# Low-part score products of a head pair contracted over 64 rows each, in a two-layer encoder trunk

## The chip, the cores and the metric

The kernel runs on one core of a Trainium2 chip. The metric is device time in microseconds (us) of one launch; the kernel before was timed three times. The profile is of one further execution, taken by the hardware profiler; its span runs from the first instruction to the last. Engines are named as the profile names them: PE is TensorE's matmuls and PEld its weight loads, DVE is VectorE, ACT ScalarE, POOL GpSimd, and SP the engine that issues most of the transfers.

## What is computed

The reference is a two-layer encoder trunk on 512 tokens of width 1024, in float32. Layer A mixes tokens with a four-head matrix memory (mLSTM) and with cross-attention to 256 memory tokens; layer B has chunked band attention with twelve heads of 64, and the same kind of memory cross-attention. Each layer ends with a gated MLP with a causal convolution. The change concerns the scores of the two attentions:

```python
def memory_attention(q, mem, w_kv):
    ...
    s = jnp.einsum('bshd,bmhd->bhsm', q, mk).astype(jnp.float32) * (MEM_HEAD_DIM ** -0.5)
    p = jax.nn.softmax(s, axis=-1).astype(mv.dtype)
    return jnp.einsum('bhsm,bmhd->bshd', p, mv).reshape(bsz, seq, MEM_WIDTH)

def band_attention(q, k_pad, v_pad, rel_table):
    ...
        s = jnp.einsum('bqhd,bkhd->bhqk', qc, kc).astype(jnp.float32) * scale + bias
        valid = (start - KV_PAD + kj) >= 0
        s = jnp.where(valid, s, -jnp.inf)
        p = jax.nn.softmax(s, axis=-1).astype(vc.dtype)
        return jnp.einsum('bhqk,bkhd->bqhd', p, vc)
```

Heads have 64 channels, so two heads share the 128 rows of a tile.

## The kernel before

**Numbers in two parts.** All products run on float32r operands. To keep float32's accuracy each operand x is held as a high part (x rounded to float32r) and a low part (x minus the high part). A full product of two operands a and b is then three matmuls into the same bank: high a with high b, high a with low b, low a with high b. mm3 (lines 176 to 180) does this; lines 178, 179 and 180 issue most of the kernel's matmuls.

**Scores of a head pair.** For 64-channel heads two of the three are put into one matmul of 128 rows. head_keys (line 504) makes for each head h a tile whose 64 rows of that head hold the high parts of the keys, and whose other 64 rows hold their low parts. head_queries (line 494) makes two tiles for each head. The first has the high parts of the queries in both halves, so that one matmul gives high times high plus high times low. The second has the low parts in the head's own rows; the other half is filled with zeros by GpSimd (line 497), so that a 128-row matmul adds low times high alone. HEADS is the pair of row ranges, 0 to 63 for head 0 and 64 to 127 for head 1. head_scores (line 511) issues the two matmuls of one head, at line 517; both load queries (or keys) as weights and accumulate in one PSUM bank.

**Who calls it.** scores (line 550) takes a head pair and two banks and calls head_scores for head 0, then for head 1: high and low of head 0, high and low of head 1. The softmax step of memory_attention (line 563) calls it for each of four tiles of 128 queries, with 256 keys; there are two head pairs in each of two layers. The softmax step of band_attention (line 1306) calls it for each of four query tiles with 128, 256, 384 and 512 keys; there are six head pairs. The mLSTM heads call head_scores themselves (line 1142), for one head at a time with the keys as weights, and need the 128-row form; their queries come from head_queries too, through qk_tile (line 1082). Attention queries come through queries (line 542).

**Order.** The kernel is written with generators: weave runs an attention job step by step and between its steps calls pieces of a filler (projections, output projection), so that other matmuls stand between the steps of a softmax. The final order on each engine is set when the program is compiled, by a planner that takes instructions in program order as far as what they need is there by its own estimate; a PSUM bank or a buffer that isn't free yet lets others go first. The engines then run their lists strictly as planned. PSUM tiles of the scores have three banks (tag sc); operand tiles have 57 buffers (tag u).

Of the kernel before, what the change touches and what calls it, by code (L numbers as in the profile page):

```python
# [46 lines left out]
def f(ap):  # L47
    return ap.bitcast(F32)
# [3 lines left out]
def trunk(  # L52
# [18 lines left out]
    nc = tc.nc  # L71
    V, A, G = nc.vector, nc.scalar, nc.gpsimd
# [10 lines left out]
    def sb(tag, shape, dtype=F32):  # L83
        count[0] += 1
        return pool.tile(shape, dtype, tag=tag, name=f"{tag}{count[0]}", bufs=bufs[tag])
# [28 lines left out]
    for i, sel in enumerate(sels):  # L114
        G.memset(f(sel), 0.0)
        for s in (2 * i, 2 * i + 1):
            q = slice(32 * s, 32 * s + AH)
# [11 lines left out]
    HEADS = (slice(0, HD), slice(HD, P))  # L129
# [3 lines left out]
    def split(hi, lo, src, on_act=True, pinned=False):  # L133
        high = A.copy(hi, src) if on_act else V.tensor_copy(hi, src)  # L134
        low = V.tensor_tensor(out=lo, in0=src, in1=f(hi), op=ALU.subtract)  # L135
        if pinned:
            pin(high)
            pin(low)
# [43 lines left out]
    def project(w, c0, act, tag="mm", lo=None):  # L182


        n = len(act)
        src = rows(w, c0, P)
        wh, wl = weights(src, n, P) if lo is None else summed_weights(lo, src, n, P)
        o = ps(tag)
        for k in range(n):
            mm3(o, wh[:, k, :], wl[:, k, :], act[k][0], act[k][1], k == 0, k == n - 1)  # L190
            yield
        return o
# [298 lines left out]

    def head_queries(t, scale=1.0):
        qs, ls = ([sb("u", [P, S], F32R) for _ in range(2)] for _ in range(2))
        for h, r in enumerate(HEADS):
            G.memset(f(ls[h])[HEADS[1 - h], :], 0.0)
            A.activation(qs[h][r, :], t[r, :], AF.Copy, scale=scale)
            V.scalar_tensor_tensor(ls[h][r, :], t[r, :], scale, f(qs[h])[r, :], op0=ALU.mult, op1=ALU.subtract)
        for h, r in enumerate(HEADS):  # L500
            A.copy(qs[h][HEADS[1 - h], :], f(qs[h])[r, :])
        return qs, ls

    def head_keys(t):
        ks = [sb("u", [P, S], F32R) for _ in range(2)]
        for h, r in enumerate(HEADS):
            A.copy(ks[h][r, :], t[r, :])
            V.tensor_tensor(out=ks[h][HEADS[1 - h], :], in0=t[r, :], in1=f(ks[h])[r, :], op=ALU.subtract)
        return ks

    def head_scores(o, h, q, tsl, k, c, first, keys_first=False):

        for i, part in enumerate(q):
            a, b = part[h][:, tsl], k[h][:, c]
            if keys_first:
                a, b = b, a
            nc.tensor.matmul(o, a, b, start=first and i == 0, stop=i == 1)  # L517
# [24 lines left out]
    def queries(o, row):  # L542

        if row is None:
            return head_queries(o, HD**-0.5)
        q = sb("t", [P, S])
        V.scalar_tensor_tensor(q, o, HD**-0.5, row, op0=ALU.mult, op1=ALU.mult)
        return head_queries(q)

    def scores(outs, q, tsl, k, c):  # L550

        for h in range(2):
            head_scores(outs[h], h, q, tsl, k, c, True)

    def memory_attention(q, kv, hp, mixes):

# [6 lines left out]
        def softmax(T2):  # L563
            ss = [ps("sc").rearrange("p (t m) -> p t m", t=2) for _ in range(2)]
            for i in range(2):
                T = 2 * T2 + i
                scores([s[:, i, :] for s in ss], q, slice(T * P, (T + 1) * P), k, slice(hp * MEM, (hp + 1) * MEM))
                yield
            for h in range(2):
                mx, sm = small(2), small(2)  # L570
                V.tensor_reduce(mx, ss[h], axis=AX.X, op=ALU.max, negate=True)
                e = sb("t", [P, S]).rearrange("p (t m) -> p t m", t=2)
                for i in range(2):
                    A.activation(e[:, i, :], ss[h][:, i, :], AF.Exp, bias=mx[:, i : i + 1], accum_out=sm[:, i : i + 1])
                V.reciprocal(sm, sm)
                for i in range(2):
                    V.tensor_scalar(e[:, i, :], e[:, i, :], sm[:, i : i + 1], None, op0=ALU.mult)
                es[T2, h] = e
                yield
# [417 lines left out]
    e, u, c, r = (cpool.tile([P, TT, AH], F32, name=f"gate{i}") for i in range(4))  # L997
# [84 lines left out]
    def qk_tile(c):  # L1082

        o = yield from project(w_in, c * P, act)
        acc = sb("t", [P, S])
        cw, cb = col["cw"], col["cb"]
        A.activation(acc, o, AF.Identity, scale=cw[:, 36 + c : 37 + c], bias=cb[:, c : c + 1])
        for i in (1, 2, 3):
            w = cw[:, 12 * (3 - i) + c : 12 * (3 - i) + c + 1]
            V.scalar_tensor_tensor(acc[:, i:], o[:, : S - i], w, acc[:, i:], op0=ALU.mult, op1=ALU.add)  # L1090
        A.activation(acc, acc, AF.Silu)
        if c % 3 == 1:
            return (head_queries if c < 6 else head_keys)(acc)
        hi, lo = sb("u", [P, S], F32R), sb("u", [P, S], F32R)
        split(hi, lo, acc)
        return hi, lo
# [14 lines left out]
    def a_tiles(*js):  # L1111
        for j in js:
            qs[j] = yield from qk_tile(j)
            ks[j] = yield from qk_tile(6 + j)
        for j in js:
            og[j] = yield from o_tile(j)
# [179 lines left out]
    def band_attention(j, q, k, v):  # L1296
# [9 lines left out]
        def softmax(T):  # L1306
            n = (T + 1) * P
            ss = [ps("sc")[:, :n] for _ in range(2)]
            scores(ss, q, slice(T * P, n), k, slice(0, n))
            for h in range(2):  # L1310
                e = sb("t", [P, S])[:, :n]
                mn, sm = small(1), small(1)
                V.tensor_tensor_reduce(
                    out=e, in0=ss[h], in1=biases[h][:, S - n :], scale=-1.0, scalar=BIG,
                    op0=ALU.add, op1=ALU.min, accum_out=mn,
                )
                A.activation(e, e, AF.Exp, bias=mn, scale=-1.0, accum_out=sm)
                V.reciprocal(sm, sm)
                V.tensor_scalar(e, e, sm, None, op0=ALU.mult)
                es[T, h] = e  # L1320
            yield
# [102 lines left out]
    for hf in range(2):  # L1424
# [6 lines left out]
        for Ts, pieces in groups:  # L1431
            for c in pieces:
                if c.start:
                    os_[Ts[0]] = ps("mm")
                for u in range(n):
# [4 lines left out]
                    for T in Ts:  # L1440
                        for i in range(2):
                            k = 2 * u + i
# [58 lines left out]
```

## Time and profile before

| what | value |
|---|---|
| median of three runs | 1211.98 us (1211.79 to 1214.2) |
| span of the profiled execution | 1209.9 us |
| matmuls at line 517 | 192, of which 160 by scores |
| memsets at line 497 | 24, of 64 x 512 elements |
| mean granted TensorE clock | 0.999 |

The page gives a line for each engine's busy time and for the chain of work that ended last. Queries of the trace give more: the busy time of each engine in stretches of the span; who waited for whom; a source line's instructions with their shortest, median and longest duration; and the timeline, where each row has its start, its duration, the engine, the line, the operation with out<-in by the program's names, the shape (rows*columns of the weights, then partitions x elements moved) and a count of merged instructions. Matmuls overlap in the pipeline, so their durations don't add up; from the start of one to the start of the next is what each costs a full TensorE.

### The profile page before, as it was taken

The numbers are of one execution on the slowest core, as the hardware profiler recorded it, in microseconds if no ns is written. First come the engines' busy times: TensorE is split into PE (matmuls) and PEld (weight loads), VectorE is DVE, ScalarE is ACT, GpSimd is POOL, SyncE is SP. The second block draws the span as 40 slices with busy tenths as digits, with TensorE's granted clock in tenths as the row PEclk, the third lists the DMA queues.
The fourth block names the chain that finished last, engine by engine and source line by source line (L and its number), as shares of the span: only waits on it lengthen the run. The fifth ranks groups of instructions, "written<-read, shape, count | busy, mean of one in ns | idle before, by whom it ended". The sixth has DMA issues, their size and how long they took to land.

```text
span 1209.9 us, 18791 instructions
## 1 busy us (share of the span) xinstructions
PE 1196.0 (99%) x7063; PEld 1058.6 (87%) x7063; DVE 945.1 (78%) x1733; ACT 711.1 (59%) x1251; POOL 125.3 (10%) x197
## 2 busy tenths in 40 slices
PE   9999999999999999999999999999999999999997
PEld 9988888888889999999988888878889999999986
DVE  7878688877978777777698888997896777777755
ACT  4536577644655555555475667775565555555545
POOL 1300000001011111111011000001101001111100
PEclk9999999999999999999999999999999999999999
DMA  8634111347556676665563323145845466666551
GB/s 276 207 98 122 54 53 57 109 138 187 129 137 160 145 160 150 161 141 133 143 195 109 99 72 94 57 129 167 199 97 139 107 138 139 140 140 134 120 156 70
DMA packets 205260, 159.14 MB, mean 132 GB/s; under 512 B 7960, under 2 KB 185586, under 8 KB 205170
## 3 DMA queue, kind: packets, MB, share of 16 engines
q1 hardware_dynamic: 184338, 120.78, 34.1%
q0 software_dynamic: 20832, 37.17, 16.5%
q8 instruction: 55, 0.90, 0.3%
q14 instruction: 35, 0.29, 0.1%
HBM read 129.42 MB, written 32.44 MB: 134 GB/s over the span
## 4 chain that ended last, share of the span: by engine, by line
PE 94%; ACT 3%; DVE 2%; issue 0%; ACTq 0%; DVEq 0%
PE pmm L178 18%; PE pmm L180 18%; PE pmm L179 18%; PE ptr L178 6%; PE ptr L179 6%; PE ptr L180 6%; PE psc L180 5%; PE psc L178 5%; PE psc L179 5%; PE psc L517 2%; PE ptr L1328 1%; ACT wh L134 1%; PE ptr L1349 1%; PE ptr L1350 1%; PE ptr L586 0%; PE ptr L600 0%
## 5 line engine op out<-in xcount | busy, mean ns | idle before, releaser
L178 PE MATMUL pmm<-u,wh 128*128 128x512 f32 (+1 forms) x968 | 337.1, 349 | 0.1
L180 PE MATMUL pmm<-u,wl 128*128 128x512 f32 (+1 forms) x968 | 333.6, 345 | 0.0
L179 PE MATMUL pmm<-u,wh 128*128 128x512 f32 (+1 forms) x968 | 333.3, 345 | 0.1
L135 DVE TENSOR_TENSOR wl<-wr,wh 128x1024 fp32r<-128x1024 f32 (+4 forms) x168 | 194.7, 1160 | 96.7 <-ACT wh L134 96.0
L134 ACT CAST wh<-wr 128x1024 fp32r<-128x1024 f32 (+4 forms) x168 | 168.0, 1002 | 99.9 <-PE pmm L179 47.2
L180 PEld LDWEIGHTS pmm<-u,wl 128*128 128x128 f32 x968 | 183.6, 190 | 21.1
L179 PEld LDWEIGHTS pmm<-u,wh 128*128 128x128 f32 x968 | 183.9, 190 | 18.0 <-DVE u L135 0.8
L178 PEld LDWEIGHTS pmm<-u,wh 128*128 128x128 f32 x968 | 183.7, 190 | 17.7 <-ACT u L134 0.5
L178 PE MATMUL ptr<-u,wh 128*128 128x512 f32 x272 | 106.7, 392 | 0.0
L179 PE MATMUL ptr<-u,wh 128*128 128x512 f32 x272 | 106.5, 392 | 0.0
L180 PE MATMUL ptr<-u,wl 128*128 128x512 f32 x272 | 105.8, 389 | 0.0
L748 POOL DMA_DIRECT2D xspill<-t x64 | 56.0, 875 | 411.4 <-ACT t L747 408.6
L178 PE MATMUL pmm<-u,u 128*128 128x256 f32 x296 | 84.5, 285 | 2.5 <-ACT t L824 2.5
L180 PE MATMUL pmm<-u,u 128*128 128x256 f32 x296 | 84.0, 284 | 0.4 <-DVE u L135 0.4
L179 PE MATMUL pmm<-u,u 128*128 128x256 f32 x296 | 83.8, 283 | 0.0
L135 DVE TENSOR_TENSOR u<-pt,u 128x512 fp32r<-128x512 f32 x102 | 69.9, 688 | 9.7 <-ACT u L134 7.1
L178 PE MATMUL psc<-u,wh 128*128 128x256 f32 (+1 forms) x232 | 76.1, 328 | 0.0
L179 PE MATMUL psc<-u,wh 128*128 128x256 f32 (+1 forms) x232 | 75.9, 327 | 0.0
L747 ACT COPY t<-ptr 128x512 f32<-128x512 f32 x64 | 37.5, 586 | 65.3 <-PE ptr L180 65.3
L135 DVE TENSOR_TENSOR u<-t,u 128x512 fp32r<-128x512 f32 x78 | 53.4, 689 | 21.4 <-ACT u L134 21.1
L134 ACT CAST u<-pt 128x512 fp32r<-128x512 f32 x102 | 63.2, 619 | 11.4 <-DVE pt L859 11.1
L921 ACT ACTIVATE t<-t 128x512 f32<-128x512 f32 x34 | 21.6, 635 | 80.2 <-DVE t L657 80.2
(290 smaller groups left out, 2568.0 us busy)
## 6 DMA issues: line engine op xcount, KB each, us to landing
wr<-in_ffn_w_up_dram SPq DMA_DIRECT2D x54, 512.0 KB, 5.0
wr<-in_ffn_w_down_dram SPq DMA_DIRECT2D x38, 512.0 KB, 3.8
pt<-in_ffn_w_up_dram SPq DMA_DIRECT2D x34, 512.0 KB, 6.8
xspill<-t POOLq DMA_DIRECT2D x64, 256.0 KB, 4.8
wr<-in_a_w_in_dram SPq DMA_DIRECT2D x20, 512.0 KB, 3.8
xspill<-u POOLq DMA_DIRECT2D x32, 256.0 KB, 3.0
u<-xspill SPq DMA_DIRECT2D x32, 256.0 KB, 4.9
wr<-in_w_kv_dram SPq DMA_DIRECT2D x12, 512.0 KB, 4.1
```

The lines of the kernel that those rows point to most:

```text
L134: high = A.copy(hi, src) if on_act else V.tensor_copy(hi, src)
L135: low = V.tensor_tensor(out=lo, in0=src, in1=f(hi), op=ALU.subtract)
L178: nc.tensor.matmul(o, lh, rh, start=first, stop=False, skip_group_check=more)
L179: nc.tensor.matmul(o, lh, rl, start=False, stop=False, skip_group_check=more)
L180: nc.tensor.matmul(o, ll, rh, start=False, stop=last, skip_group_check=more)
L517: nc.tensor.matmul(o, a, b, start=first and i == 0, stop=i == 1)
L747: A.copy(t, o)
L748: G.dma_start(xspill[j], t, accum_op=ALU.add)
L921: A.activation(self.acc, self.acc, AF.Silu)
L1328: nc.tensor.transpose(tp[:, b * P : (b + 1) * P], es[T, h][:, b * P : (b + 1) * P], ident)
L1349: nc.tensor.matmul(o2[:, s * P :], w, hi_at(pts[h], s, s, TT - s), start=s == 0, stop=False)
L1350: nc.tensor.matmul(o2[:, s * P :], w, lo_at(pts[h], s, s, TT - s), start=False, stop=s == TT - 1)
```

## The change

In scores the two high products now come first, on 128 rows as before, each into its own bank. Behind them come the two low products, one for each head, on that head's 64 rows alone: rows 0 to 63 for head 0, rows 64 to 127 for head 1, both of the queries' low part and of the key tile. Since the other half of a low tile is then not read, head_queries fills it with zeros only when it is asked to (whole=True), which the mLSTM queries in qk_tile still do.

```diff
-    def head_queries(t, scale=1.0):
+    def head_queries(t, scale=1.0, whole=False):
         qs, ls = ([sb("u", [P, S], F32R) for _ in range(2)] for _ in range(2))
         for h, r in enumerate(HEADS):
-            G.memset(f(ls[h])[HEADS[1 - h], :], 0.0)
+            if whole:
+                G.memset(f(ls[h])[HEADS[1 - h], :], 0.0)
             A.activation(qs[h][r, :], t[r, :], AF.Copy, scale=scale)
             V.scalar_tensor_tensor(ls[h][r, :], t[r, :], scale, f(qs[h])[r, :], op0=ALU.mult, op1=ALU.subtract)
...
     def scores(outs, q, tsl, k, c):
 
         for h in range(2):
-            head_scores(outs[h], h, q, tsl, k, c, True)
+            nc.tensor.matmul(outs[h], q[0][h][:, tsl], k[h][:, c], start=True, stop=False)
+        for h, r in enumerate(HEADS):
+            nc.tensor.matmul(outs[h], q[1][h][r, tsl], k[h][r, c], start=False, stop=True)
...
         if c % 3 == 1:
-            return (head_queries if c < 6 else head_keys)(acc)
+            return head_queries(acc, whole=True) if c < 6 else head_keys(acc)
```

## The prediction, made before the changed kernel was built or run

> **What bounds the kernel now.** I read the page first, then busy time by stretches, then who made TensorE wait.
>
> ```profile
> span 1209.9 us, 18791 instructions
> PE 1196.0 (99%) x7063; PEld 1058.6 (87%) x7063; DVE 945.1 (78%) x1733; ACT 711.1 (59%) x1251; POOL 125.3 (10%) x197
> PE 94%; ACT 3%; DVE 2%; issue 0%; ACTq 0%; DVEq 0%
> ```
>
> TensorE is busy for 99% of the span and holds 94% of the chain that ended last. All score products lie between 60 and 250 us (layer A) and between 640 and 820 us (layer B), so I asked for those two stretches (columns: stretch, length, then busy time of PE, PEld, DVE, ACT, POOL), and for TensorE's longest wait.
>
> ```profile
> 60.00:250.00 190.00, 189.90 (x982) 161.73 (x982) 143.95 (x287) 117.67 (x199) 3.12 (x6) 1.00 0.29 83
> 640.00:820.00 180.00, 179.38 (x931) 149.16 (x930) 155.12 (x390) 125.13 (x288) 13.42 (x24) 1.00 0.32 93
> PE pmm L178 <- ACT t L824: 2.5, 4, 0.7
> ```
>
> The two stretches hold 0.1 and 0.6 us of idle TensorE, at the full granted clock (1.00); its longest wait, 2.5 us in all, lies outside both. So nothing there hides time added to TensorE, and time saved there is saved on the path. The change is to be priced from start to start of matmuls, not by the duration of one, because they overlap.
>
> **What the score products cost now.** L517 issues 192 products; 32 belong to the mLSTM heads and stay, 160 belong to 40 calls of scores(), four each: 24 calls in band attention (6 pairs, N = 128, 256, 384, 512) and 16 in memory attention (2 layers, 2 pairs, 4 row tiles, N = 256). The timeline of pair j = 0 shows the four products of a call merged in one row, and the row behind says when they were through.
>
> ```profile
> L517 PE MATMUL psc<-u,u x192: 220/283/498, 108.3 to 814.6; 128*128 128x256 f32 x96, 128*128 128x512 f32 x32, 128*128 128x384 f32 x32, 128*128 128x128 f32 x32
> 653.59 0.69 PE L517 MATMUL psc<-u,u 128*128 128x128 f32 x4
> 654.12 0.45 PE L178 MATMUL pmm<-u,wh 128*128 128x512 f32 x1
> ...
> 654.87 0.63 PE L517 MATMUL psc<-u,u 128*128 128x256 f32 x4
> 655.34 0.40 PE L178 MATMUL pmm<-u,wh 128*128 128x512 f32 x1
> ...
> 658.31 0.88 PE L517 MATMUL psc<-u,u 128*128 128x384 f32 x4
> 659.03 0.39 PE L178 MATMUL pmm<-u,wh 128*128 128x512 f32 x1
> ...
> 661.57 1.08 PE L517 MATMUL psc<-u,u 128*128 128x512 f32 x4
> 662.49 0.39 PE L178 MATMUL pmm<-u,wh 128*128 128x512 f32 x1
> ```
>
> From start to start a call takes 0.53, 0.47, 0.72 and 0.92 us. Half of it, the two low products, is 0.265, 0.235, 0.36 and 0.46 us: 1.32 us for a pair of heads in band attention, 0.235 us for a call in memory attention. A product alone streams for 0.23 us at N = 512, so 0.06, 0.12, 0.17 and 0.23 us by width.
>
> **The change part by part.** (1) The two low products contract 64 rows each and stand behind each other. If they ran wholly side by side, a call would save one product: 0.13, 0.12, 0.18, 0.23 us by width, 0.66 us a band pair. 6 x 0.66 + 16 x 0.12 = 5.9 us is the most that the change can bring.
>
> (2) What does it cost to use part of the rows? Before has no product on 64 rows. The nearest place is the transposes on 4 rows at L1075 and L1076, amid 128-row products (first fence matmuls, second weight loads).
>
> ```profile
> 99.15 0.39 PE L179 MATMUL pmm<-u,wh 128*128 128x512 f32 x1
> 99.38 0.39 PE L180 MATMUL pmm<-u,wl 128*128 128x512 f32 x1
> 99.70 0.22 PE L1075 MATMUL ptr<-ident,t 4*128 4x4 f32 x1
> 99.78 0.20 PE L1076 MATMUL ptr<-ident,t 4*128 4x4 f32 x1
> ...
> 100.15 0.20 PE L1076 MATMUL ptr<-ident,t 4*128 4x4 f32 x1
> 100.28 0.50 PE L178 MATMUL pmm<-u,wh 128*128 128x512 f32 x1
> 100.62 0.39 PE L179 MATMUL pmm<-u,wh 128*128 128x512 f32 x1
> ```
>
> ```profile
> 99.16 0.19 PEld L180 LDWEIGHTS pmm<-u,wl 128*128 128x128 f32 x1
> 99.70 0.13 PEld L1075 LDWEIGHTS ptr<-ident,t 4*128 4x128 f32 x1 [0.35 <-issue]
> 99.75 0.14 PEld L1076 LDWEIGHTS ptr<-ident,t 4*128 4x128 f32 x1
> ...
> 100.28 0.19 PEld L178 LDWEIGHTS pmm<-u,wh 128*128 128x128 f32 x1
> 100.39 0.19 PEld L179 LDWEIGHTS pmm<-u,wh 128*128 128x128 f32 x1
> ```
>
> Among 128-row products the next weights load while the last product streams: L180's load starts at 99.16, beside L179's product of 99.15. Not so on the way in: L180 has streamed by 99.38 + 0.23 = 99.61, and the first 4-row load starts only at 99.70, after 0.09 us in which the engine waited for nothing that the profile shows. On the way out the last small product takes its step of 0.06 us from 100.15; the load for L178 starts at 100.28, 0.07 us later, and is exposed: L179 follows at 100.62, so L178 streamed from 100.39, 0.11 us behind its load. From 99.38 to 100.62 are 1.24 us; less two products of 0.23 us and eight steps of 0.0625 us, **0.28 us went for the way in and out**.
>
> The Trainium skill, "TensorEngine Tiling (Array Packing)", section Key Properties, says that a change of the tiling mode, not just of the tile, drains TensorE. It gives no time for it; the trace agrees, with the gaps of 0.09 and 0.07 us, and by these the sum comes out above the time before.
>
> That small rows are not enough for such a gap shows at L323, whose transpose contracts 106 rows:
>
> ```profile
> 32.49 0.62 PE L254 MATMUL psc<-t,onesr 128*128 128x512 f32 x2
> 32.95 0.26 PE L323 MATMUL ptr<-ident,t 106*128 106x106 f32 x1
> 32.98 0.37 PE L178 MATMUL pmm<-wh,u 128*128 128x256 f32 x1
> 33.18 0.28 PE L179 MATMUL pmm<-wl,u 128*128 128x256 f32 x1
> ```
>
> Two products of 0.23 us end at 32.95, and L323 starts there: no gap. Whether 64 rows behave as 4 or as 106 is the open point. Rows 64 to 127 cannot stand at the top of the array, and the change wants the halves side by side, so I take them to behave as 4.
>
> (3) The load itself is dearer here than at L1075, which transposes plain float32. The queries are float32r:
>
> ```profile
> L517 PEld LDWEIGHTS psc<-u,u x192: 186/188/192, 108.0 to 814.4; 128*128 128x128 f32 x192
> L586 PEld LDWEIGHTS ptr<-ident,t x64: 138/141/143, 175.0 to 803.7; 128*128 128x128 f32 x64
> ```
>
> At equal shape a float32r load takes 188 ns, a float32 one (L586) 141. So I don't take the 0.06 us steps of the 4-row stretch but the 0.11 us between the loads of 100.28 and 100.39.
>
> (4) The sum for a call: 0.09 in, 0.11 for the first low load, 0.11 for the second, the stream of the second product, 0.07 and 0.11 out: **0.49 us plus the stream**, so 0.55, 0.61, 0.66 and 0.72 us by width, in place of 0.265, 0.235, 0.36 and 0.46. A band pair takes 2.54 - 1.32 = 1.22 us more, a memory call 0.375 us more. 6 x 1.22 + 16 x 0.375 = 7.3 + 6.0 = **13.3 us more**. The lower bound of the slow case takes the 4-row stretch as it is: 0.28 + 0.06 + stream, 0.15 us less in each of 40 calls, 7.3 us more.
>
> (5) Calls that are cut. The compiled order sets other products between the two heads of a call; first and last of nine such calls:
>
> ```profile
> 162.17 0.40 PE L517 MATMUL psc<-u,u 128*128 128x256 f32 x2
> 162.64 0.40 PE L517 MATMUL psc<-u,u 128*128 128x256 f32 x2
> ...
> 805.51 0.40 PE L517 MATMUL psc<-u,u 128*128 128x256 f32 x2
> 807.35 0.40 PE L517 MATMUL psc<-u,u 128*128 128x256 f32 x2
> ```
>
> If a call's low products are parted too, each goes in and out alone: 2 x (0.38 + 0.12) = 1.0 us instead of 0.61, 0.39 more, 3.5 us for nine. The new order may wait for both banks instead; I count nothing and keep 3.5 us for the upper end.
>
> (6) GpSimd loses 20 of 24 memsets (minimum, median, maximum in ns behind the count).
>
> ```profile
> L497 POOL MEMSET u<- x24: 518/522/660, 47.8 to 765.4; 64x512 f32 x24
> L499 DVE SCALAR_TENSOR_TENSOR u<-t,u x20: 665/686/692, 97.0 to 788.0; 64x512 fp32r<-64x512 f32 x20
> ```
>
> That is 20 x 0.52 = 10.4 us of an engine that is busy for 125.3 us. TensorE's longest wait is on ScalarE and short, so I cost it at nothing. The buffer's release is then awaited by VectorE's subtraction instead of the memset; with VectorE busy for 155.12 of 180 us in layer B, that falls in its slack or behind work it would do anyway. Without that cover each of the 10 query sets could delay its scores by the subtraction of L499, 0.69 us; TensorE has other products to do meanwhile, so nothing. The second high product now stands ahead of the first low one, so head 0's scores are ready up to 0.23 us later; VectorE reads them with other work queued, nothing again.
>
> **The sum.** 1209.9 + 13.3 = 1223.2 us of span. The runs' median, 1211.98, is 2.1 us above the profiled span; with these around it, 1225.3, say **1225 us**.
>
> **The rivals.** (a) Faster: the halves load and stream side by side and there is no gap. Place: the same 40 calls; price: the 5.9 us of (1) saved, 1206.1 us. For it: the two heads write different banks and read different rows. Against it: the stretch at 99.38. It decides where way in and out together with the second load cost under 5.9 / 40 = 0.15 us a call; the 4-row stretch says 0.34.
>
> The Trainium skill, "TensorE: Matmul & The Clock Gate", section Measured speedup vs the span model, gives packed matmuls one duration plus about 4 ns for each further tile. By that estimate 40 x 0.004 = 0.16 us of the 5.9 are lost, and the time is 1206.2 us; no 64-row product of this trace bears on it.
>
> (b) No gap, but the two loads follow each other at 0.11 us: a call's low part takes 0.11 us plus the stream, 0.17, 0.23, 0.28 and 0.34 us. That saves 0.30 us a band pair and nothing at a memory call: 1.8 us, 1210.2 us. For it: loads never stand closer than about 0.11 us in the float32r rows above.
>
> (c) The change doesn't do what it says: 64-row products pass as 106-row ones did, one behind the other at full price; 1212 us.
>
> **How the numbers follow.** The forecast has 0.76 (the only row in the trace with few rows in 128-row surroundings shows gaps both ways), (a) 0.14, (b) and (c) 0.05 each. 0.2% is 2.4 us and about what a measurement of this kernel can tell from no change. Faster 0.14, same 0.10, slower 0.76. The slow case alone reaches from 1219.3 (bound of (4)) to 1228.8 (all nine calls parted) and some 3 us above, where other parts of the order shift. The range that leaves out no more than 2 in 10 takes in (b), (c) and the edge of (a): 1207 to 1232.
>
> **What would show it.** In the trace of after: low products as 64-row rows at L555 or so, 80 of them. Right: before the first low load of a call TensorE stands idle for about 0.09 us, its load does not overlap the high product, and the 128-row load after the pair starts after the pair's stream; a call at N = 256 takes about 0.85 us instead of 0.47. (a) shows the two low products starting within a few ns and the next 128-row load beside them, (b) loads at 0.11 us with no gap, (c) 0.47 us as before. Wrong would be the sum if the drain for 64 rows is shorter than for 4, if the load of 64 rows takes less than 0.11 us, or if the planner parts many more calls. POOL's busy time should fall by some 10 us without any effect.

## The result and the profile after

The changed kernel took 1226.15 us (median of four runs, 1225.52 to 1226.34), the kernel before on the same chip 1212.42 us. The ratio is 1.011, with a 95% interval of 1.0097 to 1.0124: **slower by 13.7 us**, where 1225 us and 13.3 us more were forecast. The profiled spans say the same, 1223.6 against 1209.9 us.

The head of the page after:

```profile
span 1223.6 us, 18731 instructions
PE 1209.8 (99%) x7063; PEld 1058.2 (86%) x7063; DVE 946.1 (77%) x1733; ACT 710.7 (58%) x1251; POOL 113.9 (9%) x177
PE 94%; ACT 3%; DVE 2%; issue 0%; ACTq 0%; DVEq 0%
```

TensorE runs as many matmuls as before, 7063, and is busy for 13.8 us more, the whole loss. GpSimd lost its 20 memsets and 11.4 us of busy time, and nobody gained by it. The other engines' busy times moved by 1 us or less. Where the time went shows in one call, pair j = 0 with 384 keys, first TensorE's matmuls, then its weight loads (start, duration, engine, line, operation, shape, count):

```profile
663.42 0.39 PE L180 MATMUL pmm<-u,wl 128*128 128x512 f32 x1
663.64 0.51 PE L554 MATMUL psc<-u,u 128*128 128x384 f32 x2
664.08 0.44 PE L556 MATMUL psc<-u,u 64*128 64x384 f32 x2
664.45 0.50 PE L178 MATMUL pmm<-u,wh 128*128 128x512 f32 x1
664.79 0.39 PE L179 MATMUL pmm<-u,wh 128*128 128x512 f32 x1
```

```profile
663.42 0.42 PEld L554 LDWEIGHTS psc<-u,u 128*128 128x128 f32 x2
664.08 0.19 PEld L556 LDWEIGHTS psc<-u,u 64*128 64x128 f32 x2 [0.25 <-issue]
664.45 0.19 PEld L178 LDWEIGHTS pmm<-u,wh 128*128 128x128 f32 x1 [0.18 <-issue]
664.56 0.19 PEld L179 LDWEIGHTS pmm<-u,wh 128*128 128x128 f32 x1
```

Read it from start to start. The two high products take 0.44 us; two streams of 0.175 us are 0.35, so **0.09 us** are lost on the way in. The two low products cover 0.44 us together, as long as one of them lasts, and their two loads 0.19 us, as long as one load: they do run side by side. But from their start to the next product's load are 0.37 us, **0.20 us** more than one stream of 0.17: their own load, no longer hidden, and a second gap (one of the experiments parts the two). The load of L178 then starts no earlier than its product, so L178 takes 0.34 us instead of 0.23, **0.11 us** more. A trip in and out costs 0.40 us and one stream. Before, this call's four products and the step behind them took 0.72 + 0.23 us; now it is 0.44 + 0.37 + 0.34, 0.20 us more.

Not all calls kept their two low products together:

```profile
167.32 0.28 PE L554 MATMUL psc<-u,u 128*128 128x256 f32 x1
167.53 0.38 PE L556 MATMUL psc<-u,u 64*128 64x256 f32 x1
167.84 0.50 PE L178 MATMUL pmm<-u,wh 128*128 128x512 f32 x1
```

Here head 0's low product goes in and out alone, and head 1's two products follow 2 us later. On the timeline 28 calls are whole and 12 are cut: 28 + 24 = 52 trips for 40 calls.

### The profile page after: what moved, and what is told of

Its sections match the earlier page's. It is cut to its first block, busy times and chain, and to the rows that moved or that the text cites. A ratio compares the mean times of both kernels' runs of the same rounds, so it can differ in the third digit from the quotient of the medians.

```text
span 1223.6 us, 18731 instructions
## 1 busy us (share of the span) xinstructions
PE 1209.8 (99%) x7063; PEld 1058.2 (86%) x7063; DVE 946.1 (77%) x1733; ACT 710.7 (58%) x1251; POOL 113.9 (9%) x177
## 4 chain that ended last, share of the span: by engine, by line
PE 94%; ACT 3%; DVE 2%; issue 0%; ACTq 0%; DVEq 0%
PE pmm L178 18%; PE pmm L180 18%; PE pmm L179 17%; PE ptr L178 6%; PE ptr L179 6%; PE ptr L180 6%; PE psc L178 5%; PE psc L180 5%; PE psc L179 5%; PE psc L556 1%; PE psc L554 1%; PE ptr L1331 1%; PE ptr L1352 1%; ACT wh L134 1%; PE ptr L1353 1%
## 5 line engine op out<-in xcount | busy, mean ns | idle before, releaser
L178 PE MATMUL pmm<-u,wh 128*128 128x512 f32 (+1 forms) x968 | 340.8, 352 | 0.1
L179 PE MATMUL pmm<-u,wh 128*128 128x512 f32 (+1 forms) x968 | 333.2, 344 | 0.1
L178 PEld LDWEIGHTS pmm<-u,wh 128*128 128x128 f32 x968 | 183.6, 190 | 22.6 <-issue 2.2
L179 PEld LDWEIGHTS pmm<-u,wh 128*128 128x128 f32 x968 | 183.8, 190 | 18.1 <-DVE u L135 0.8
L178 PE MATMUL ptr<-u,wh 128*128 128x512 f32 x272 | 106.7, 392 | 0.0
L179 PE MATMUL ptr<-u,wh 128*128 128x512 f32 x272 | 106.5, 392 | 0.0
L178 PE MATMUL pmm<-u,u 128*128 128x256 f32 x296 | 84.5, 285 | 2.5 <-ACT t L827 2.5
L179 PE MATMUL pmm<-u,u 128*128 128x256 f32 x296 | 83.8, 283 | 0.0
L178 PE MATMUL psc<-u,wh 128*128 128x256 f32 (+1 forms) x232 | 76.1, 328 | 0.0
L179 PE MATMUL psc<-u,wh 128*128 128x256 f32 (+1 forms) x232 | 75.9, 327 | 0.0
```

What stands on the lines that cost most here:

```text
L178: nc.tensor.matmul(o, lh, rh, start=first, stop=False, skip_group_check=more)
L179: nc.tensor.matmul(o, lh, rl, start=False, stop=False, skip_group_check=more)
```

## The experiments

Theory: a trip between 128-row and 64-row products costs 0.40 us, with one stream for each pair of low products in it (or for a single one). Rivals: the moved order, the memsets, a price for each product, a price for whatever has fewer rows. All ratios are to the kernel before, run beside each kernel (1211.75 to 1212.42 us). Differences of about 1 us between kernels have to be read with care: in the profiled executions the 386th matmul starts between 60.0 and 61.3 us, long before the first call of scores, so the score products can't have made these differences.

The diffs are to the changed kernel unless another is named, and "..." marks what is left out. pin holds an instruction in program order, so that the planner can't move it. In "order alone", "96 rows", "one head" and "widest calls only" the memsets are kept too, by the edit shown under "Memsets kept"; their diffs leave it out.

| kernel | median us | ratio (95% interval) | trips |
|---|---|---|---|
| changed | 1226.15 | 1.011 (1.0097 to 1.0124) | 52 |
| order alone | 1213.39 | 1.0014 (1.0006 to 1.0023) | 0 |
| 96 rows | 1212.96 | 1.0010 (1.0001 to 1.0019) | 0 |
| paired | 1221.69 | 1.0079 (1.0066 to 1.0091) | 40 |
| one head on 64 rows | 1226.97 | 1.0124 (1.0109 to 1.0140) | 40 |
| low products twice | 1227.85 | 1.0130 (1.0116 to 1.0143) | 41 |
| batched | 1218.40 | 1.0049 (1.0036 to 1.0062) | 32 |
| alone | 1238.19 | 1.0215 (1.0201 to 1.0229) | 80 |
| changed, memsets kept | 1229.15 | 1.0140 (1.0125 to 1.0156) | 56 |
| paired, memsets kept | 1220.16 | 1.0065 (1.0051 to 1.0079) | 40 |
| widest calls only | 1213.64 | 1.0012 (1.0003 to 1.0021) | 6 |

**Order alone.**

```diff
...
-        for h, r in enumerate(HEADS):
-            nc.tensor.matmul(outs[h], q[1][h][r, tsl], k[h][r, c], start=False, stop=True)
+        for h in range(2):
+            nc.tensor.matmul(outs[h], q[1][h][:, tsl], k[h][:, c], start=False, stop=True)
```

> Order alone: the two high products first, then the two low ones, all on 128 rows, memsets kept. Mode theory (TensorE drains and loses its overlapped weight load each time it goes between 128-row and 64-row products; a trip in and out costs 0.40 us plus one stream): nothing of that is here, so the time of before, 1212.4 us, within 1 us. Rival, order theory (the loss comes from the low products having moved behind the second head's high product, and from the planner's new list): most of the 13.7 us stay, 1220 to 1226 us.

1213.39 us, 1.6 us above before: the order is not where the 13.7 us went. The expectation of 1 us was missed by a little. The two traces have the same list of matmuls up to 657 us, yet in the first 60 us, long before any score product, this one is already behind (first the kernel before, then this one; busy time and count of PE, PEld, DVE, ACT and POOL):

```profile
0.00:60.00 60.00, 56.61 (x385) 54.43 (x386) 48.71 (x115) 29.87 (x48) 13.58 (x43) 1.00 0.75 241
0.00:60.00 60.00, 55.10 (x378) 53.12 (x379) 48.04 (x112) 29.08 (x46) 13.58 (x43) 1.00 0.74 240
```

It is through 378 matmuls there, the kernel before through 385; the 100th matmul already starts 1.2 us later. So of the 1.9 us between the two profiled spans 1.2 us have another source than the order of the scores; which one stays open.

**96 rows.**

```diff
...
-        for h, r in enumerate(HEADS):
-            nc.tensor.matmul(outs[h], q[1][h][r, tsl], k[h][r, c], start=False, stop=True)
+        for h, r in enumerate((slice(0, 96), slice(0, P))):
+            pin(nc.tensor.matmul(outs[h], q[1][h][r, tsl], k[h][r, c], start=False, stop=True))
```

> As the kernel with one head on 64 rows, but head 0's low product contracts rows 0 to 95 (32 of them zeros). Mode theory, with the whole array used as soon as a product has more than 64 rows, as 106 rows showed in the trace of before: no trip, 1212.4 us within 1 us. Rival (any product on fewer rows than its neighbours stops the loads from running ahead): 40 trips, about 1228 us.

1212.96 us, as forecast. The timeline shows no gap at all (the merged row is one product on 96 rows and one on 128):

```profile
162.42 0.40 PE L254 MATMUL psc<-t,onesr 128*128 128x512 f32 x1
162.65 0.40 PE L555 MATMUL psc<-u,u 96*128 96x256 f32 x2
162.89 0.40 PE L178 MATMUL pmm<-u,wh 128*128 128x512 f32 x1
163.12 0.40 PE L179 MATMUL pmm<-u,wh 128*128 128x512 f32 x1
```

0.23 us for the 512-wide product, 0.24 for two of 256, 0.23 for the next. So fewer rows alone don't cost; 64 of them do. Where between 64 and 88 rows (the fewest without a gap in the trace of before, at L323) the border lies, no run shows.

**One head on 64 rows.** The same edit with slice(0, HD) in place of slice(0, 96).

> As the paired kernel, but only head 0's low product is on 64 rows (rows 0 to 63); head 1's is on 128 rows with its zeros, memsets kept. So nothing runs side by side, and there are 40 trips. Mode theory: 40 x 0.40 = 16 us above before, 1228.4 us; the distance to the paired kernel, some 6 us, is what running side by side is worth. Rival (the price comes from two products side by side, or from rows 64 to 127 not being at the top of the array): 1212 us, as before.

1226.97 us. No two products run side by side and none stands in rows 64 to 127, but the 40 trips are there, at (1226.97 - 1211.81) / 40 = 0.38 us. That excludes both forms of the rival. Against the paired kernel, next, side by side is worth 5.3 us. That kernel has no memsets and this one has; against the paired kernel with its memsets kept, at the end, it is 6.8 us.

**Paired.**

```diff
         for h, r in enumerate(HEADS):
-            nc.tensor.matmul(outs[h], q[1][h][r, tsl], k[h][r, c], start=False, stop=True)
+            pin(nc.tensor.matmul(outs[h], q[1][h][r, tsl], k[h][r, c], start=False, stop=True))
```

> The changed kernel, with each call's two low products held behind both high ones and next to each other, so that no call is cut: 40 trips in place of the 52 of the changed kernel's trace. Mode theory: 12 trips fewer at 0.40 us, and 12 streams of 0.06 to 0.12 us fewer, 4.8 + 1.3 = 6.1 us less than 1226.2: 1220.1 us, and 1222.4 by adding 40 trips to before. Rival (the price is one for each 64-row product, of which there are 80 either way): 1226 us, unchanged or above by waits for the second bank.

1221.69 us, between the two numbers of the theory, with 40 trips in the trace. The 12 cut calls had cost 4.5 us by the medians, 3.9 us if each is taken against the kernel before run beside it: some 30% of the loss.

**Low products twice.** The scores count the low parts twice. The diff is to the paired kernel.

```diff
-        for h, r in enumerate(HEADS):
-            pin(nc.tensor.matmul(outs[h], q[1][h][r, tsl], k[h][r, c], start=False, stop=True))
+        for i in range(2):
+            for h, r in enumerate(HEADS):
+                pin(nc.tensor.matmul(outs[h], q[1][h][r, tsl], k[h][r, c], start=False, stop=i == 1))
```

> The paired kernel with each call's two low products issued twice in a row, so the low parts count twice in the scores. It prices one more pair inside a trip, against the paired kernel. If the two halves load and stream side by side: 0.11 us (128 columns, bound by the load), 0.12, 0.175, 0.23 us a call, 5.7 us in all. Rival, loads one behind the other at 0.11 us: 0.22 to 0.23 us a call, about 9 us. Rival, each pair drains anew: 0.40 us more a call, 21 us.

6.2 us more than paired, 5.7 forecast; one call is cut here (41 trips), and a trip is worth 0.4 us. The call with 384 keys, the second pair alone from a narrower window, and the four weight loads:

```profile
663.18 0.62 PE L557 MATMUL psc<-u,u 64*128 64x384 f32 x4
663.73 0.50 PE L178 MATMUL pmm<-u,wh 128*128 128x512 f32 x1
663.46 0.34 PE L557 MATMUL psc<-u,u 64*128 64x384 f32 x2
663.18 0.30 PEld L557 LDWEIGHTS psc<-u,u 64*128 64x128 f32 x4 [0.25 <-issue]
```

Four low products take 0.55 us from start to start where two took 0.37: a second pair costs 0.18 us, one stream. Inside a trip there is no gap, and loads of the two halves don't follow each other at 0.11 us: the fourth would then start 0.33 us after the first, but all four are over after 0.30. The row of the second pair also parts the 0.20 us that the low products of a call lose. It starts 0.28 us after the first pair, a load of 0.11 and a stream of 0.17; from there to L178 are 0.27 us, a stream and a gap of **0.09 us** on the way out.

**Batched.** Two query tiles' low products in memory attention share a trip; band attention is as in the paired kernel (cut from the diff, as are the slices c and tsl).

```diff
...
-            for i in range(2):
-                T = 2 * T2 + i
-                scores([s[:, i, :] for s in ss], q, slice(T * P, (T + 1) * P), k, slice(hp * MEM, (hp + 1) * MEM))
-                yield
+            for i in range(2):
+                for h in range(2):
+                    hi = nc.tensor.matmul(ss[h][:, i, :], q[0][h][:, tsl[i]], k[h][:, c], start=i == 0, stop=False, ...)
+                    if i or h:
+                        pin(hi)
+            for i in range(2):
+                for h, r in enumerate(HEADS):
+                    pin(nc.tensor.matmul(ss[h][:, i, :], q[1][h][r, tsl[i]], k[h][r, c], start=False, stop=True, ...))
+            yield
+            yield
```

> The paired kernel, but in memory attention the four high products of two query tiles come first and their four low products behind them: 8 trips in place of 16. Mode theory: 8 x 0.40 = 3.2 us less than the paired kernel. Rival (a price for each product or each pair, not for the trip): as the paired kernel.

3.3 us less than paired for 8 trips fewer, 0.41 us a trip. This is the cleanest price of a trip: the same products on the same rows, in an order with fewer changes between 128 and 64 rows. It is still 6.6 us slower than before.

**Alone.**

```diff
-        for h in range(2):
-            nc.tensor.matmul(outs[h], q[0][h][:, tsl], k[h][:, c], start=True, stop=False)
         for h, r in enumerate(HEADS):
-            nc.tensor.matmul(outs[h], q[1][h][r, tsl], k[h][r, c], start=False, stop=True)
+            nc.tensor.matmul(outs[h], q[0][h][:, tsl], k[h][:, c], start=True, stop=False)
+            pin(nc.tensor.matmul(outs[h], q[1][h][r, tsl], k[h][r, c], start=False, stop=True))
```

> The order of before (high and low of head 0, then high and low of head 1), but each low product on its own 64 rows: every low product goes in and out alone, 80 trips, nothing side by side. Mode theory: 80 x 0.40 = 32 us above before, 1244 us, some us less where a wait of before already stood. Rival (a price for each call, or for products that stand side by side): 1228 us or less.

1238.19 us, 26.4 us above before: far above the rival, and 5.6 us short of 80 x 0.40. To see where those are, I took from the step of every matmul, start to start, the median step of a product of its width in the kernel before (0.227, 0.174, 0.120 and 0.109 us for 512, 384, 256 and 128 columns), and added up the rest. At the low products and their two neighbours it is 30.1 us; at all others it is 19.1 us, while the kernel before has 22.7 us in all. So the trips cost nearly what they should (80 x 0.38), and 3.6 us of other delays of before are gone; that these short waits now fall into the longer steps is an argument that no run tests. In the changed kernel the same two sums are 16.0 and 20.4 us: 16.0 more at the low products and their neighbours and 2.3 less elsewhere are its 13.7 us.

**Memsets kept, in the changed kernel and in the paired one.**

```diff
-            if whole:
-                G.memset(f(ls[h])[HEADS[1 - h], :], 0.0)
+            G.memset(f(ls[h])[HEADS[1 - h], :], 0.0)
```

> The changed kernel with all 24 memsets kept. If the memsets were hidden, as I costed them: the changed kernel's time, 1226.2 us within 1 us, with GpSimd's busy time back at about 125 us. Rival (taking the memsets out moved a wait for the buffer onto VectorE, which costs time, or saved some): a difference of over 2 us either way.

1229.15 us, 3.0 us above the changed kernel: this missed. The trace has 56 trips in place of 52, since the planner, given 20 more instructions, cut four more calls. At 0.40 us and a lost stream each that is some 2 us, and 0.9 us more stand in the first 60 us of the trace, before any call of scores (its 386th matmul starts at 60.9 us, that of the changed kernel at 60.0). Whether the memsets themselves cost anything the next kernel tells, in which no call is cut:

> The paired kernel with all 24 memsets kept. The changed kernel with its memsets kept took 3 us more than without, with 56 trips in place of 52 in its trace. Theory: the memsets cost nothing themselves; they moved the planner's order, which cut four more calls. With no call cut, the time is that of the paired kernel, 1221.7 us within 1 us. Rival (taking the memsets out saves time by itself, by GpSimd's port or by VectorE's waits): some 3 us more, 1224.7 us.

1220.16 us, 1.5 us below the paired kernel without memsets, not 3 above; the 1 us of the expectation was missed, on the other side. So the memsets cost nothing, and taking them out gained nothing. Of the 1.3 us between the two profiled spans, 0.7 us lie in the first 60 us, before any call of scores; why this one is faster stays open.

**Widest calls only.**

```diff
...
+        wide = c.stop - c.start == S
         for h, r in enumerate(HEADS):
-            nc.tensor.matmul(outs[h], q[1][h][r, tsl], k[h][r, c], start=False, stop=True)
+            r = r if wide else slice(0, P)
+            low = nc.tensor.matmul(outs[h], q[1][h][r, tsl], k[h][r, c], start=False, stop=True)
+            if wide:
+                pin(low)
```

> Only the widest calls (512 keys, 6 of the 40) have their low products on 64 rows, paired; all others as in the run of the order alone. Here a pair saves most: one stream of 0.23 us against a trip of 0.40 us. Mode theory with the measured trip: 6 x 0.17 = 1.0 us above the order alone (1213.4), 1214.4 us. Rival (wide pairs gain, the narrow ones lose): 6 x 0.23 = 1.4 us below it, 1212.0 us.

1213.64 us, 0.25 us above the order alone, with intervals that overlap: by the time alone the two expectations, 1.0 us above and 1.4 below, can't be told apart. The traces tell them apart. The same call of pair j = 0, first with the order alone, then here:

```profile
663.00 0.63 PE L553 MATMUL psc<-u,u 128*128 128x512 f32 x2
663.46 0.62 PE L555 MATMUL psc<-u,u 128*128 128x512 f32 x2
663.92 0.39 PE L178 MATMUL pmm<-u,wh 128*128 128x512 f32 x1
664.15 0.40 PE L179 MATMUL pmm<-u,wh 128*128 128x512 f32 x1
```

```profile
661.99 0.62 PE L553 MATMUL psc<-u,u 128*128 128x512 f32 x2
662.54 0.49 PE L557 MATMUL psc<-u,u 64*128 64x512 f32 x2
662.97 0.50 PE L178 MATMUL pmm<-u,wh 128*128 128x512 f32 x1
663.31 0.40 PE L179 MATMUL pmm<-u,wh 128*128 128x512 f32 x1
```

From the first high product to L179 are 1.15 us with the order alone and 1.32 us here, 0.17 us more, as the theory has it. Summed as under "Alone", the low products of the six calls and their neighbours take 1.0 us more than their median steps. So even the best case of the change, a stream of 0.23 us saved a call, loses. None of the kernels beats the one before.

## Why the prediction was right

**What bounds it.** Right: TensorE's busy time grew by 13.8 us, the span by 13.7; nothing hid it.

**The gap on the way in and out.** Right in kind, and in size on the way in: 0.09 us at L1075 before, 0.09 us at L556 after. On the way out 0.07 us had been read, and the kernel with the low products twice shows 0.09. That 64 rows behave as 4 and not as 106 was the open point; the 96-row and one-head kernels settle it.

**The low loads.** The 0.11 us of the first one were right, but not for the reason given, the type of the operands. At L586, which transposes plain float32 on 128 rows, the trace of before has steps of 0.11 us too, and not the 0.06 us of the 4-row products. On the chain that ended last four of them take 0.44 us:

```profile
175.42 0.44 PE ptr L586 x4
```

The second load was wrong: the sum had 0.11 us for each of two loads, and the loads of the two halves go together. A whole call costs 0.40 us plus the stream, not 0.49; over 40 calls 3.6 us too many. It shows in the sign that had been named, 0.85 us for a call at N = 256:

```profile
659.91 0.40 PE L554 MATMUL psc<-u,u 128*128 128x256 f32 x2
660.23 0.39 PE L556 MATMUL psc<-u,u 64*128 64x256 f32 x2
660.55 0.49 PE L178 MATMUL pmm<-u,wh 128*128 128x512 f32 x1
660.88 0.39 PE L179 MATMUL pmm<-u,wh 128*128 128x512 f32 x1
```

The call takes 0.64 us and makes the step of L178 0.10 us longer: 0.74 us.

**Cut calls.** Wrong the other way: nothing was counted and 3.5 us kept for nine calls at the upper end. Twelve calls were cut, and the paired kernel shows that they cost 3.9 to 4.5 us. The two errors nearly cancel by luck, so the 1225 us are nearer than their terms are: without cut calls the sum should have come to the paired kernel's 9.9 us, not 13.3.

**Memsets and VectorE's wait.** Right that they cost nothing; not foreseen was that they move the planner's list.

**The rivals.** (a) was right that the halves run side by side, worth 5.3 us against the one-head kernel (6.8 us with memsets in both) where at most 5.9 had been worked out; it fell by the trip, 0.40 us against the 0.15 at which it would have decided. The Trainium skill's few nanoseconds for a further tile ("TensorE: Matmul & The Clock Gate", Measured speedup vs the span model) agree: the two low products of a whole call with 384 keys cover 0.44 us in the rows of the result, and each alone lasts as long. The Trainium skill's rule on draining ("TensorEngine Tiling (Array Packing)", Key Properties) agrees with what decided, here 0.40 us a trip in gaps and exposed loads. (b) fell with the loads, (c) with the gaps.

## What to carry to other kernels

Before halving the rows of a few products, price the way in and out, not only the streams: here one trip costs 0.40 us, as much as almost two 512-wide products, so two products side by side can't pay for it. It is a price for each trip: put everything that can run on half rows in one place, and hold it together against the planner, which cut 12 of 40 calls. How much has to share a trip before it gains, no run shows; at 0.40 us a trip and 0.12 us saved by a pair of 256 columns, four such pairs are an estimate, and the batched kernel had two. A single odd place in a trace, eight tiny transposes here, can carry such a price if its neighbours' steps are read from start to start.

## What the runs showed of the hardware that was not expected

The weight loads of the two halves run together, and two of them take 0.19 us, as long as one (the load rows of the call with 384 keys). Inside a trip a second pair's loads are hidden again: four low products of 384 columns take 0.55 us. And 96 rows cost the same as 128, with no gap, while 64 rows cost a trip, which the prediction had left open.
